# A short-convolution block on one core: two late operand forms split straight from PSUM, transposes of the second half spread between products, five late low parts spaced out

## The chip, the cores and the metric

The kernel runs on one core of a Trainium2 chip. The metric is the device time of one execution in microseconds. The median of three runs of the kernel before is 780.94 us (780.88 to 781.16).

## The reference, cut to what matters

The inputs are x of 1024 frames by 1024 channels, two norm weights, `w_in` (1024 x 8192), three taps for each of 2048 channels, and `w_out` (2048 x 1024), all float32. There is one layer, and its mixer is the short convolution:

```python
u = rms_norm(x, pre_norm)
z, bg, cg, v = jnp.split(u @ w_in, 4, axis=-1)      # 4 x 2048 columns
y = bg * causal_dwconv(cg * v, conv_w) * jax.nn.silu(z)
out = x + rms_norm(y @ w_out, post_norm)
```

## The kernel before, in words

**Precision.** Every float32 operand of a matmul is split into a high part (a rounded copy, made by ScalarE) and a low part (operand minus high part, made by VectorE or GpSimd). `pass3` (lines 122 to 125) multiplies low by high, high by low and high by high into one PSUM bank. So one product over one block of 128 input channels is three matmuls of 512 columns.

**The products.** The 64 column groups of `w_in` (16 channel blocks times four types: CG, V, Z, BG) are worked off in this way: the first four, called plain, by full products (`plain`, lines 511 to 521: 8 blocks of channels for each half of the frames, 24 matmuls for one group and half, accumulated in a bank `pp`). The other 60 are taken in 20 triples by a bilinear scheme: 20 products `product(t, i)` of six matmuls each replace the larger number of direct ones. The normalized and transposed x is held as eight blocks B[g, h] (g: four groups of 256 channels, h: two halves of 512 frames). Each of the 20 products has its own left operand, U[i]: seven products use a block B itself (lines 756 and 757; five blocks serve them), the other thirteen use "forms", sums and differences of blocks. A form is built once at the start, split into high and low, and used by all 20 triples.

**Where a form is built.** `form(i, ...)` (line 550) and `banks_of(i)` (line 718) build a form in two PSUM banks; `stage(i)` (line 538) is a place in SBUF for forms that are finished later. `high_u(i)` (line 555) allocates the operand tile u_i and makes the high part on ScalarE; `low_u(i)` (line 563) makes the low part on VectorE, or on GpSimd if told so. Each reads the form from its banks as long as it is listed in `FORM`, else from SBUF (line 569 instead of 567). `keep(i)` (line 578) copies a form from its banks to its staging place, so that the banks come free. Before the change forms 6 and 11 are kept in that way and split in the product loop; form 8 is one addition of two SBUF blocks (line 694).

**Order.** The order is written out by hand; each engine takes its instructions in that order. Lines 668 to 760 are the part that the change touches: while TensorE works on the plain products, x of the second half is transposed by TensorE in pairs of blocks (`turn2`, line 530, eight matmuls of 128 columns for a pair), read out with scale and split into B[g, 1] (`read_k`, line 473: line 479 on ScalarE, line 480 on VectorE), combined into staged forms (`turned`, line 585, issued at line 588), and written back as plain float32 (`rebuild_a`, line 488). `snap` (line 523) reads a finished plain bank with ScalarE.

The loop over triples (line 822) issues for each of 20 positions s: the six matmuls of one product, `read` of its bank (line 334: the first read of a group is a copy by ScalarE, lines 345 and 347, later ones an add or subtract by VectorE, lines 351 and 353), the outstanding low parts of weights (`run_lows`; lines 218 to 224 are the split of a unit of two weight operands, with the unit's name in the tile: wA to wJ), outstanding low parts of forms (`low_us`), and only in the first triple `first_chunk` and the late forms: at odd s one of `LATE` gets its high part, and its low part is issued one position later. The first triple's order of products is `ORDER_0` (line 820): 7, 9, 1, 8, 3, 5, 14, 18, 0, 13, 17, 6, 4, 11, 15, 16, 10, 2, 12, 19. Products of one chain (line 127: X, Y, V, Z, W) accumulate in one bank and are read in between, so a product waits for the reads of the chain's product before it.

**Space.** There are 8 PSUM banks (line 58), taken in turn as they come free, for transposes, plain sums, forms, weight splits and chains alike. The pool `up` has 18 slots (line 56). It holds the eight blocks B, the split plain weights wn0 to wn3 (`high_w`, line 503; each free after the plain products of its group on both halves), the operands u_i and four staging tiles s_0 to s_3, each with two forms (`PLACE`, line 536: 10 and 4, 0 and 16, 6 and 17, 11 and 2). In the end all 18 slots hold operands of products. The split weights' tiles and others of the product loop take the memory of the head's tiles xa and xb (line 741 closes that pool), so the first write to them waits for the last reader of xa, which is the building of form 2 at line 735.

## Time and profile before

| | |
|---|---|
| Median of three runs | 780.94 us (780.88 to 781.16) |
| The profiled execution's own time | 780.58 us |
| Its span, first to last instruction | 778.8 us |
| Mean granted TensorE clock over the span | 0.996 |
| Instructions | 10028 |

The span leaves 1.78 us of the profiled execution's time around it. The profile names engines PE (TensorE's matmuls), PEld (its weight loads), DVE (VectorE), ACT (ScalarE), POOL (GpSimd) and SP (SyncE). A row of the timeline has the start in us from the span's start, the duration, engine and line, output and inputs by the program's names, the number of merged instructions, and in brackets the idle time before them with what ended it. Matmul durations are of pipelined instructions, so two rows in turn overlap; their starts tell the pace.

### The profile page before, as it was taken

How to read it: one execution, taken by the hardware profiler on the slowest of the kernel's cores; microseconds unless marked ns; L12 is line 12 of the kernel's file. 1: busy time of each engine (PE TensorE's matmuls, PEld its weight loads, DVE VectorE, ACT ScalarE, POOL GpSimd, SP SyncE). 2: the span in 40 equal slices, each digit the busy share in tenths (PEclk: the TensorE clock that was granted, in tenths of full speed). 3: DMA queues.
4: the chain of work that ended last, by engine and by line, in shares of the span. 5: the costliest groups of instructions: out<-in, count | busy, mean ns of one | idle time of the engine just before them, and what ended most of it. 6: DMA issues, size and time to landing. Idle time of an engine off the chain costs nothing.

```text
span 778.8 us, 10028 instructions
## 1 busy us (share of the span) xinstructions
PE 763.1 (98%) x3394; PEld 629.3 (81%) x3394; DVE 490.6 (63%) x752; ACT 451.2 (58%) x879; POOL 460.0 (59%) x563
## 2 busy tenths in 40 slices
PE   8989899999999999999999999999999999999996
PEld 8877688888888888888888888888888888888885
DVE  6897865655566465656565665555664957544756
ACT  7749565666556566645665755565565636544531
POOL 0688487678669669676977986796884320000020
PEclk9999999999999999999999999999999999999999
DMA  9400325545535446356267366565544779754237
GB/s 331 131 0 28 108 68 163 121 125 138 144 96 162 135 109 187 82 156 151 79 138 195 76 177 128 147 159 113 129 104 133 233 241 375 282 189 176 99 118 260
DMA packets 103219, 116.55 MB, mean 150 GB/s; under 512 B 4680, under 2 KB 70272, under 8 KB 102144
## 3 DMA queue, kind: packets, MB, share of 16 engines
q1 hardware_dynamic: 93936, 99.13, 38.6%
q0 software_dynamic: 9216, 16.78, 13.8%
q8 instruction: 26, 0.43, 0.2%
q14 instruction: 25, 0.20, 0.1%
q10 hardware_dynamic: 16, 0.00, 0.0%
HBM read 97.02 MB, written 44.04 MB: 181 GB/s over the span
## 4 chain that ended last, share of the span: by engine, by line
PE 88%; ACT 6%; DVE 5%; issue 1%; DMA 0%; DVEq 0%; ACTq 0%
PE pX L123 8%; PE pX L125 8%; PE pX L124 8%; PE pY L123 7%; PE pY L124 7%; PE pY L125 7%; PE po_x L887 4%; PE po_x L886 4%; PE po_x L885 4%; PE pV L123 3%; PE pV L125 3%; PE pV L124 3%; PE pZ L123 2%; PE pZ L124 2%; PE pZ L125 2%; PE pW L123 2%
## 5 line engine op out<-in xcount | busy, mean ns | idle before, releaser
L925 POOL TENSOR_TENSOR res<-xr,res 128x512 f32<-128x512 f32 x4 | 6.9, 1720 | 105.4 <-DVE res L924 105.4
L329 POOL TENSOR_TENSOR g<-g,sn 128x512 f32<-128x512 f32 x29 | 40.1, 1390 | 46.0 <-ACT sn L327 35.4
L353 DVE TENSOR_TENSOR sn<-sn,pY 128x512 f32<-128x512 f32 x57 | 39.2, 688 | 35.9 <-PE pY L125 21.6
L353 DVE TENSOR_TENSOR sn<-sn,pX 128x512 f32<-128x512 f32 x57 | 39.2, 688 | 34.9 <-PE pX L125 34.9
L302 POOL TENSOR_TENSOR g<-sn,g 128x512 f32<-128x512 f32 x23 | 29.8, 1298 | 47.8 <-DVE sn L351 47.8
L327 ACT ACTIVATE sn<-sn 128x512 f32<-128x512 f32 x24 | 15.2, 632 | 64.1 <-DVE sn L353 40.1
L311 POOL TENSOR_TENSOR g<-g,sn 128x512 f32<-128x512 f32 x20 | 28.2, 1411 | 17.7 <-DVE sn L353 17.4
L345 ACT COPY sn<-pZ 128x512 f32<-128x512 f32 x19 | 11.2, 588 | 46.6 <-PE pZ L125 46.6
L347 ACT ACTIVATE sn<-pV 128x512 f32<-128x512 f32 x38 | 20.7, 599 | 28.6 <-PE pV L125 28.6
L169 POOL TENSOR_TENSOR raw<-raw 128x256 f32<-128x256 f32 x40 | 32.5, 929 | 0.0
L359 POOL DMA_DIRECT2D s_d<-s_d x24 | 19.8, 823 | 21.0 <-DMA s_d<-y_d 13.5
L174 POOL TENSOR_TENSOR raw<-e,raw 128x256 f32<-128x256 f32 x40 | 29.2, 751 | 1.6
L351 DVE TENSOR_TENSOR g<-pY,g 128x512 f32<-128x512 f32 x15 | 10.4, 692 | 30.7 <-PE pY L125 30.7
L123 PE MATMUL pp<-b,wn 128*128 128x512 f32 x64 | 25.9, 405 | 2.1 <-ACT b L479 1.8
L170 POOL TENSOR_TENSOR e<-raw,raw 128x512 f32<-128x512 f32 x20 | 25.8, 1292 | 1.6
L894 ACT ACTIVATE jk<-res 128x512 bf16<-128x512 f32 x12 | 7.6, 632 | 31.9 <-DVE res L952 13.0
L124 PE MATMUL pp<-b,wn 128*128 128x512 f32 x64 | 25.2, 394 | 0.6 <-DVE b L480 0.6
L125 PE MATMUL pp<-b,wn 128*128 128x512 f32 x64 | 25.0, 390 | 0.0
L292 DVE SCALAR_TENSOR_TENSOR g<-g,cw,cv 128x512 f32<-128x512 f32 x30 | 22.5, 749 | 1.7
L224 DVE TENSOR_TENSOR wD<-wD,wD 128x512 fp32r<-128x512 f32 x20 | 13.7, 685 | 14.8 <-ACT wD L223 14.8
L181 POOL TENSOR_TENSOR e<-e,raw 128x256 f32<-128x256 f32 x20 | 14.8, 740 | 13.9 <-ACT wB L219 13.9
L292 DVE SCALAR_TENSOR_TENSOR cv<-g,cw,cv 128x512 f32<-128x512 f32 x30 | 22.4, 748 | 0.0
(373 smaller groups left out, 2910.0 us busy)
## 6 DMA issues: line engine op xcount, KB each, us to landing
raw<-in_sc_w_in SPq DMA_DIRECT2D x64, 512.0 KB, 4.4
t_d<-in_sc_w_out SPq DMA_DIRECT2D x32, 256.0 KB, 4.3
s_d<-g SPq DMA_DIRECT2D x29, 256.0 KB, 2.1
s_d<-s_d POOLq DMA_DIRECT2D x24, 256.0 KB, 4.4
y_d<-g SPq DMA_DIRECT2D x23, 256.0 KB, 2.5
t_d<-in_sc_w_out POOLq DMA_DIRECT2D x16, 256.0 KB, 7.8
t_d<-t_d POOLq DMA_DIRECT2D x16, 256.0 KB, 4.3
xr<-in_x SPq DMA_DIRECT2D x8, 512.0 KB, 4.9
```

The lines of the kernel that those rows point to most:

```text
L123: nc.tensor.matmul(ps, lo, u[:, 0, kk], start=first, stop=False, skip_group_check=True)
L124: nc.tensor.matmul(ps, hi, u[:, 1, kk], start=False, stop=False, skip_group_check=True)
L125: nc.tensor.matmul(ps, hi, u[:, 0, kk], start=False, stop=last, skip_group_check=True)
L169: 0: lambda: (add(w2[:, 0], w2[:, 0], w2[:, 1]), add(w2[:, 2], w2[:, 1], w2[:, 2])),
L174: 5: lambda: (sub(w0[:, 2], e[:, 3], w0[:, 2]), sub(w0[:, 0], e[:, 3], w0[:, 0])),
L292: nc.vector.scalar_tensor_tensor(g if j == TAPS - 1 else ps, g, tap(c, j), ps, op0=ALU.mult, op1=ALU.add)
L302: nc.gpsimd.tensor_mul(g, src, g)
L329: when([(c, "cv", h), (c, "silu", h)], (c, "z", h), {"cv": 1, "silu": 1}, lambda: nc.gpsimd.tensor_mul(cv_of(c, h), cv_of(c, h), t))
L353: nc.vector.tensor_sub(a, a, ps)
L885: nc.tensor.matmul(ps, lo, u[:, 0, k % 2], start=first, stop=False, skip_group_check=True)
L886: nc.tensor.matmul(ps, hi, u[:, 1, k % 2], start=False, stop=False, skip_group_check=True)
L887: nc.tensor.matmul(ps, hi, u[:, 0, k % 2], start=False, stop=last, skip_group_check=True)
```

## The change

Form 8 gets its two banks earlier (`banks_of` moves up). ScalarE copies b20 (block of group 2, first half) into them, VectorE adds b00 in place, and high and low part follow at once, ahead of the transposes of the second half. The plain product of group 3 on the first half is no longer cut in two; it runs whole before the first pair of transposes. After each pair come products that need only blocks already read.

Forms 6 and 11 are no longer kept in SBUF: their high parts are made from the banks at once, the low part of 6 as soon as form 2 is staged, the low part of 11 behind the split of weight unit B. High and low part of form 0 move behind the first four weight units. The late list has five forms, 4, 16, 10, 2 and 19, at s = 4, 7, 10, 12 and 14, where there were seven at s = 1, 3, 5, 7, 9, 11 and 13.

```diff
@@ -578,6 +578,10 @@
+    def banks_of(i):
+        FORM[i] = [bank(f"f_{i}_{kk}") for kk in range(2)]
+        return in_bank(i)
@@ -673,17 +677,23 @@
     low_u(7)
     high_u(9)
     form(5, turned(4, gneg, b00, ALU.subtract), [pk[4, 1], pk[5, 1]])
+    f8 = banks_of(8)
+    for kk in range(2):
+        nc.scalar.copy(f8[kk], b20[:, kk])
     low_u(9)
     sn0[2] = snap(2, 0)
     high_u(5)
-    plain(3, 0, range(KH))
+    make(nc.vector, f8, "+", f8, b00)
+    low_u(5)
+    high_u(8)
+    low_u(8)
+    plain(3, 0, range(NK))
     turn2((0, 1))
     for k in (0, 1):
         read_k(k, 1)
     for kk in range(2):
         turned(0, gneg, b00, ALU.add)(stage(10)[:, kk], kk)
-    low_u(5)
-    plain(3, 0, range(KH, NK))
+    plain(0, 1, (4, 5))
     turn2((6, 7))
     for k in (0, 1):
         rebuild_a(k, 1)
@@ -691,20 +701,17 @@
         read_k(k, 1)
     for kk in range(2):
         turned(6, gcol, b30, ALU.subtract)(stage(4)[:, kk], kk)
-    form(8, lambda dst, kk: nc.vector.tensor_add(dst, b00[:, kk], b20[:, kk]))
+    plain(1, 1, (4, 5))
+    plain(0, 1, (0, 1))
+    turn2((2, 3))
     sn0[3] = snap(3, 0)
-    plain(0, 1, (4, 5, 0, 1))
-    turn2((2, 3))
-    high_u(8)
     for k in (6, 7):
         rebuild_a(k, 1)
-    low_u(8)
     for k in (2, 3):
         read_k(k, 1)
-    plain(0, 1, (6, 7))
-    plain(1, 1, (4, 5))
-    plain(0, 1, (2, 3))
-    plain(1, 1, (0, 1, 6, 7, 2, 3))
+    plain(1, 1, (0, 1))
+    plain(0, 1, (6, 7, 2, 3))
+    plain(1, 1, (6, 7, 2, 3))
     sums(0, range(12))
@@ -726,18 +729,18 @@
-    keep(6)
+    high_u(6)
     make(nc.vector, stage(17), "+", f6, b30)
     nc.vector.tensor_mul(cv_of(0, 1), plain_ps[1, 1], cv_of(0, 1))
     f11 = banks_of(11)
     make(nc.vector, f11, "-", f6, b00)
-    keep(11)
+    high_u(11)
     make(nc.vector, stage(2), "+", f11, b10)
-    FORM.clear()
+    FORM.pop(19)
+    FORM.pop("q")
+    low_u(6)
     nc.gpsimd.tensor_mul(inner(gts[0, 0]), inner(gts[0, 0]), sn0[1])
     pad(0)
-    high_u(0)
-    low_u(0, nc.gpsimd)
     head.close()
@@ -745,9 +748,12 @@
     for unit in "ABCD":
         split_w(0, unit)
         run_lows()
+        if unit == "B":
+            low_u(11)
     sums(0, range(12, 16))
-    high_u(17)
-    low_u(17, nc.gpsimd)
+    for i in (0, 17):
+        high_u(i)
+        low_u(i, nc.gpsimd)
     first_tap(0, 0)
@@ -755,7 +761,7 @@
-    LATE = [6, 4, 11, 16, 10, 2, 19]
+    LATE = [4, 16, 10, 2, 19]
@@ -829,7 +835,7 @@
             if t == 0:
                 first_chunk(s)
-                if s % 2 and LATE:
+                if s in (4, 7, 10, 12, 14):
                     n = LATE.pop(0)
                     high_u(n)
                     low_us.append(lambda n=n: low_u(n))
```

More of the change, by code (lines that the diff above doesn't have):

```diff
@@ L716 @@
         plain(n, 1, (4, 5, 0, 1, 6, 7, 2, 3))
-    def banks_of(i):
-        FORM[i] = [bank(f"f_{i}_{kk}") for kk in range(2)]
-        return in_bank(i)
     snap(0, 1, True)
```

## The prediction

> **What bounds the kernel now.** First the page, for shares and the chain that ended last.

> ```profile
> span 778.8 us, 10028 instructions
> PE 763.1 (98%) x3394; PEld 629.3 (81%) x3394; DVE 490.6 (63%) x752; ACT 451.2 (58%) x879; POOL 460.0 (59%) x563
> PE 88%; ACT 6%; DVE 5%; issue 1%; DMA 0%; DVEq 0%; ACTq 0%
> ```

> TensorE holds 88% of the chain; ScalarE and VectorE together hold 11%. The change removes no matmul, so only that 11% can shrink. Then the busy time by stretches, to find where it lies (columns: stretch, its length, busy time and instructions of PE, PEld, DVE, ACT and POOL, granted clock, DMA share, GB/s).

> ```profile
> 40.00:48.00 8.00, 7.72 (x41) 6.05 (x39) 7.80 (x12) 4.21 (x8) 7.84 (x9) 1.00 0.00 1
> 48.00:52.00 4.00, 2.05 (x9) 1.43 (x9) 2.95 (x5) 2.29 (x5) 4.00 (x4) 1.00 0.00 0
> 76.50:80.00 3.50, 1.34 (x6) 1.06 (x6) 3.50 (x5) 2.82 (x7) 3.38 (x6) 0.98 0.00 0
> 80.00:83.40 3.40, 3.40 (x10) 2.68 (x9) 3.40 (x5) 0.00 (x0) 3.40 (x4) 0.52 0.00 0
> 83.40:92.00 8.60, 7.21 (x30) 5.04 (x28) 7.55 (x12) 4.44 (x8) 3.78 (x4) 1.00 0.36 132
> 99.00:776.00 677.00, 672.66 (x2962) 555.32 (x2961) 411.48 (x617) 381.26 (x750) 402.63 (x498) 1.00 0.55 154
> ```

> From 99 us TensorE is full. Its holes lie at 48 to 52, at 76.5 to 80, in a half-clock stretch right behind, and up to 92 us: in the very part that the change touches. Then TensorE's own timeline.

> ```profile
> 33.69 0.39 PE L123 MATMUL pp<-b,wn 128*128 128x512 f32 x1
> 41.35 0.50 PE L123 MATMUL pp<-b,wn 128*128 128x512 f32 x1 [0.28 <-DVE u L567]
> 49.68 0.49 PE L123 MATMUL pp<-b,wn 128*128 128x512 f32 x1 [1.66 <-ACT b L479]
> 50.47 0.50 PE L124 MATMUL pp<-b,wn 128*128 128x512 f32 x1 [0.29 <-DVE b L480]
> 66.68 0.39 PE L123 MATMUL pV<-u,wA 128*128 128x512 f32 x1
> 72.12 0.39 PE L123 MATMUL pY<-b,wC 128*128 128x512 f32 x1
> 75.97 0.39 PE L125 MATMUL pV<-b,wD 128*128 128x512 f32 x1
> 78.66 0.50 PE L123 MATMUL pX<-b,wD 128*128 128x512 f32 x1 [2.30 <-DVE g L351]
> 85.37 0.50 PE L123 MATMUL pY<-u,wE 128*128 128x512 f32 x1 [0.71 <-ACT u L561]
> 89.06 0.50 PE L123 MATMUL pY<-u,wF 128*128 128x512 f32 x1 [0.67 <-DVE gc L353]
> 98.25 0.50 PE L123 MATMUL pX<-b,wJ 128*128 128x512 f32 x1
> ```

> Products begin at 66.68; 41 starts later it is 75.97, so a matmul costs 0.2266 us and a product of six 1.36. Product 18 waits until 78.66 for the read of product 5, product 17 until 85.37, and product 12, the last but one of the triple, starts at 98.25. Whatever the change gains is the amount by which that last start moves: nothing after it waits.

> VectorE's and ScalarE's rows say why.

> ```profile
> 33.37 1.28 DVE L567 TENSOR_TENSOR u<-f,u 128x512 fp32r<-128x512 f32 x2
> 44.68 2.58 DVE L694 TENSOR_TENSOR f<-xa 128x512 f32<-128x512 f32 x2
> 50.98 1.41 DVE L588 SCALAR_TENSOR_TENSOR f_q<-pk,gcol,xb 128x512 f32<-128x512 f32 x2
> 59.30 1.29 DVE L576 TENSOR_TENSOR s<-f,xa 128x512 f32<-128x512 f32 x2
> 72.35 5.06 DVE L569 TENSOR_TENSOR u<-s,u 128x512 fp32r<-128x512 f32 x4
> L569 DVE TENSOR_TENSOR u<-s,u x4: 1067/1218/1784, 72.3 to 76.2; 128x512 fp32r<-128x512 f32 x4
> 82.21 2.50 DVE L569 TENSOR_TENSOR u<-s,u 128x512 fp32r<-128x512 f32 x2
> 84.64 0.68 DVE L224 TENSOR_TENSOR wE<-wE,wE 128x512 fp32r<-128x512 f32 x1
> 90.66 1.28 DVE L569 TENSOR_TENSOR u<-s,u 128x512 fp32r<-128x512 f32 x2
> ...
> 32.44 2.04 ACT L559 CAST u<-f 128x512 fp32r<-128x512 f32 x4
> 34.50 1.28 ACT L527 ACT_TABLE_LOAD   x1
> 37.23 1.29 ACT L479 ACTIVATE b<-pk,gcol 128x512 fp32r<-128x512 f32 x2
> 41.32 1.26 ACT L479 ACTIVATE b<-pk,gcol 128x512 fp32r<-128x512 f32 x2
> 48.93 1.28 ACT L479 ACTIVATE b<-pk,gcol 128x512 fp32r<-128x512 f32 x2
> 61.55 0.59 ACT L223 CAST wA<-wA 128x512 fp32r<-128x512 f32 x1
> 68.24 1.09 ACT L347 ACTIVATE gc<-pV 128x512 f32<-128x512 f32 x2
> 84.75 1.14 ACT L561 CAST u<-s 128x512 fp32r<-128x512 f32 x2 [5.30 <-DVE u L569]
> ...
> 68.80 1.43 POOL L169 TENSOR_TENSOR raw<-raw 128x256 f32<-128x256 f32 x2
> 71.56 3.02 POOL L764 TENSOR_TENSOR sp<-sp,sp 128x512 f32<-128x512 f32 x2
> ```

> A subtraction from PSUM takes 1.28 for two halves (33.37). With both operands in SBUF it takes as little once GpSimd rests (90.66), but 2.50 (82.21) or 5.06 for four halves (72.35) while GpSimd works; so does the addition of form 8 (44.68, 2.58). [...]

> **The change part by part.** The walk uses the profiled execution's times. Pitches: 0.60 for VectorE in a pair (1.28 has one overlap), 0.66 with a scale (1.41), 0.51 for a copy by ScalarE (2.04 for four).

> *Form 8 early.* Gone are two additions of 2.58 together and ScalarE's wait for them. Added are two copies (2 x 0.51; SBUF to PSUM, between 0.49 and 0.62 each by the weight splits' like rows) and two additions into PSUM (2 x 0.60; up to 1.29 each if they too met GpSimd, which nothing that reads one PSUM operand does in the trace). ScalarE: high part of 9 done 34.48, copies 35.5, table load 36.8, snap 37.3, high of 5 38.35, high of 8 39.4. VectorE: form 5 done 35.9 (34.57 + 2 x 0.66), low of 9 37.1, additions 38.3, low of 5 39.5, low of 8 40.7. All this lies beside 24 plain matmuls (5.44 us); without that cover it would cost about 2 us.

> *A bank.* There are eight. Form 8 now takes the two that come free first: that of the transposed taps and the first of form 7. The plain sum of group 3 gets the second of form 7, free only when its low part ends, 33.37 + 1.28 = 34.65. TensorE would be there at 33.69 as now. **New wait: 1.0 us**; bounds 0 (another bank) and 3.8 (the bank of the sum before, read by snap until 37.5).

> *Transposes.* TensorE: 34.7 + 0.1 for the restart + 5.44 = 40.24 for the first pair, which ScalarE reads from 40.9. A pair costs the ping-pong of ScalarE and VectorE: read, low parts, staged form, write back, next read: 1.29 + 1.41 + 1.41 with their gaps, 4.09 from the read at 37.23 to the next pair's at 41.32. So the third pair is read at 40.9 + 2 x 4.09 = 49.1, against 48.93: nothing is won on that chain, as it starts later. But TensorE then has fewer matmuls left, for six of group 1 went ahead. Its second matmul on that pair comes 1.54 after the read (50.47 - 48.93), at 50.62, with 64 to follow before the products instead of 70: products can begin at 50.62 + 0.33 + 64 x 0.2266 = **65.46, a gain of 1.2**. On the other side of the pair, VectorE's chain of forms starts at 51.13, 0.15 late.

> *Forms 6 and 11.* The copies that kept them become high parts of the same length. VectorE's low parts, 2 x 1.2 us, fall where it idles now, between 60.6 and 66.3. But u_6 and u_11 now take two of the 18 slots before the staging tiles of 17 and 2. Free by then: B[2,0], wn0, wn1, wn2 in that order. Form 2 gets the fourth, wn2, free when the plain sum of group 2 ends on the second half: 24 matmuls before the products, 65.46 - 5.44 + 0.2 = 60.25. VectorE would have come at 59.45 (59.30 + 0.15). So form 2 ends at 61.55, and the third copy of unit A on ScalarE, which writes where form 2's operand lies, waits for it until 61.6, against 60.7 that it could (form 0's high part, 1.04, no longer stands ahead). ScalarE then runs without a pause: A, B, C, D, high of 0 and 17, the taps. Its two copies of product 7's bank come at 69.35 instead of 68.24. **Product 8 waits for them until 70.45, and product 3 starts at 72.0 against 72.12 now: the 1.2 is spent, 0.1 is left.** Bounds: no wait for a slot, 0.95 more gain; another slot, below.

> GpSimd makes the low part of 0 after the four sums that follow unit B, 66.3 to 68.85; product 0 needs it at 80. All of these issue no DMA; SP's later loads of weights come when raw slots free, no later than now.

> *Five late ones.* Ahead of the read of product 5 stands one low part (form 4) instead of two. ScalarE: unit F 71.75, copy 72.25, high of 4 73.3, unit G 74.35. VectorE: low of G 75.05, then low of 4. GpSimd's two long multiplications (L764), ready after the taps, sit at 74.2 to 77.2: the two halves meet them and cost 1.07 + 1.78, the least and most of the first four. End 77.9, read 78.5: **product 18 at 78.55, against 78.66.** Its wait is as long as now, so the half clock follows again: matmul starts 0.43 apart. Then: 18 ends 80.0, read 80.75, low of H 81.35, low of 16 83.85 (2.50), low of E 84.45, product 17 at **84.5 against 85.37**. The half clock on products 0 and 13 is hidden in that. From there the backlog is shorter by two low parts: read of 17 at 86.75 (needed 87.2), of 4 at 89.7 (needed 90.0), of 10 at 95.2 (needed 95.45). No wait is left: eight products from 84.5 + 0.1 give 95.45 for product 12, against 98.25.

> **Sum: 2.8 us**, 0.87 of it at product 17 and 1.9 from the waits behind it. The profiled execution's 780.58 becomes 777.8; it stands 0.36 under the median 780.94, so the forecast is **778.1**.

> [...] The trace saw the fall behind 2.30 us; the half clock lasted from 80.0 to 83.4.

> **The rivals.**

> 1. *The new waits don't come* (other bank, other slot): product 17 is 0.95 to 1.9 earlier: 777.1 down to 776.2. For it: the bank and slot order is read from code and from one wait (41.35, which names the low part that freed a bank), not seen. Chance 0.13.

> 2. *VectorE's queue stays the bound.* If the half clock begins 1.4 us sooner it falls on product 18, whose read is waited for: six matmuls at 0.43 cost 1.2. [...] If every low part in SBUF up to unit E takes 1.78 a half, it is 4 x 1.78 - 2.85 - 2.50 = 1.8. So 779.3 to 781.1. For it: product 18 keeps its wait. Against: 1.78 is the largest seen. This is also the case in which the change misses its own aim. Chance 0.22.

> 3. *Slower: form 2's staging waits for a slot that only group 3's second half frees*, if one slot fewer is free than I count. Then it starts at 65.7, not 60.25; VectorE and ScalarE stand behind it, product 7 waits, everything later shifts by 5.45: 783.5. It decides from a start later than 63.1 (60.25 + 2.8). For it: 18 slots all in use at that moment. Against: the count above leaves wn2. Chance 0.10.

> **How the numbers follow.** The forecast has 0.55, with its own range 777.2 to 779.3 (0.9 and 1.2 either way, the size of one wait). Under 0.2% (1.56 us), a measurement can't tell from no change, so faster means under 779.4: the forecast, rival 1 and 0.05 of rival 2: 0.73. Same: the rest of rival 2, 0.17. Slower: rival 3, 0.10. The range 776.4 to 780.8 leaves out rival 3, and a little of 1 and 2.

> **What would show it.** TensorE waits about 1 us near 33.7 for a low part (L567); its wait near 50 is under 0.9; VectorE waits before form 2 (the second `make` on s) for a plain matmul; product 8 waits for ScalarE's copies; product 18 waits 2 us or more; product 12 starts near 95.5; PSUM low parts take 0.64 a half. I am wrong if product 18 doesn't wait (more gain), or if the wait before form 2 reaches past 63.

## The result

The changed kernel takes 777.9 us (median of 12 runs, 776.99 to 779.28) against 780.92 us for the kernel before, run beside it. The ratio is 0.9965, with a 95% interval of 0.9955 to 0.9974: 0.35% faster. The forecast was 778.1, the range 776.4 to 780.8. (One of twelve executions of the kernel before took 1565.1 us and is in no comparison.)

The profiled execution of the changed kernel took 776.99 us, the shortest of its twelve. Its page, in the same three lines as before:

```profile
span 775.2 us, 10034 instructions
PE 761.8 (98%) x3394; PEld 628.3 (81%) x3394; DVE 486.2 (63%) x752; ACT 451.1 (58%) x877; POOL 458.4 (59%) x563
PE 91%; ACT 5%; DVE 3%; issue 1%; DMA 0%; DVEq 0%; ACTq 0%
```

TensorE's share of the chain grew by 3 points, which ScalarE and VectorE lost. The stretches in which the kernel before had its holes (columns as before: stretch, length, busy time and instructions of PE, PEld, DVE, ACT and POOL, clock, DMA, GB/s):

```profile
48.00:52.00 4.00, 3.71 (x16) 2.63 (x15) 2.66 (x5) 2.26 (x5) 4.00 (x4) 1.00 0.00 0
76.00:79.50 3.50, 1.54 (x7) 1.10 (x7) 2.82 (x3) 2.19 (x5) 3.46 (x5) 1.00 0.00 0
79.50:83.00 3.50, 3.35 (x14) 2.13 (x12) 3.12 (x5) 0.00 (x0) 3.42 (x5) 1.00 0.00 0
83.00:91.60 8.60, 8.03 (x35) 6.50 (x36) 8.05 (x13) 6.85 (x14) 5.37 (x6) 1.00 0.65 202
```

The hole near 50 us is nearly shut (3.71 of 4.00 busy, 2.05 before), the one near 77 is still open, the stretch behind it has the full clock (0.52 before), and the last one is fuller. TensorE's timeline:

```profile
34.48 0.47 PE L123 MATMUL pp<-b,wn 128*128 128x512 f32 x1 [0.95 <-DVE u L567]
50.32 0.50 PE L124 MATMUL pp<-b,wn 128*128 128x512 f32 x1 [0.29 <-DVE b L480]
65.23 0.39 PE L123 MATMUL pV<-u,wA 128*128 128x512 f32 x1
70.28 0.50 PE L123 MATMUL pV<-u,wC 128*128 128x512 f32 x1 [0.80 <-ACT gc L347]
78.18 0.50 PE L123 MATMUL pX<-b,wD 128*128 128x512 f32 x1 [1.96 <-DVE g L351]
83.57 0.50 PE L123 MATMUL pY<-u,wE 128*128 128x512 f32 x1 [0.69 <-DVE wE L224]
94.69 0.39 PE L123 MATMUL pX<-b,wJ 128*128 128x512 f32 x1
```

Here are both new waits, for a bank (34.48) and for ScalarE's copies (70.28), the old wait of product 18, a shorter one of product 17, and product 12 at 94.69 instead of 98.25. VectorE's rows, then two of ScalarE's and one of GpSimd's:

```profile
33.06 1.28 DVE L567 TENSOR_TENSOR u<-f,u 128x512 fp32r<-128x512 f32 x2
60.09 1.29 DVE L576 TENSOR_TENSOR s<-f,xa 128x512 f32<-128x512 f32 x2 [1.11 <-PE pp L125]
61.30 1.28 DVE L567 TENSOR_TENSOR u<-f,u 128x512 fp32r<-128x512 f32 x2
63.74 1.28 DVE L567 TENSOR_TENSOR u<-f,u 128x512 fp32r<-128x512 f32 x2
74.80 2.73 DVE L569 TENSOR_TENSOR u<-s,u 128x512 fp32r<-128x512 f32 x2
81.08 1.83 DVE L569 TENSOR_TENSOR u<-s,u 128x512 fp32r<-128x512 f32 x2
88.97 1.28 DVE L569 TENSOR_TENSOR u<-s,u 128x512 fp32r<-128x512 f32 x2
...
48.80 1.26 ACT L479 ACTIVATE b<-pk,gcol 128x512 fp32r<-128x512 f32 x2
61.47 0.59 ACT L223 CAST wA<-wA 128x512 fp32r<-128x512 f32 x1 [1.14 <-DVE s L576]
...
73.99 2.99 POOL L770 TENSOR_TENSOR sp<-sp,sp 128x512 f32<-128x512 f32 x2
```

The low parts of forms 6 and 11 take 1.28 from their banks (61.30 and 63.74). Form 2 waits 1.11 for a plain matmul (60.09), and unit A's third copy 1.14 for form 2 (61.47). The low part of form 4 still meets GpSimd's long multiplications (74.80: 2.73, against 1.28 for two halves at 88.97, with GpSimd at rest).

### The profile page after: what moved, and what is told of

Its sections match the earlier page's. It is cut to its first block, busy times and chain, and to the rows that moved or that the text cites. A ratio compares the mean times of both kernels' runs of the same rounds, so it can differ in the third digit from the quotient of the medians.

```text
span 775.2 us, 10034 instructions
## 1 busy us (share of the span) xinstructions
PE 761.8 (98%) x3394; PEld 628.3 (81%) x3394; DVE 486.2 (63%) x752; ACT 451.1 (58%) x877; POOL 458.4 (59%) x563
## 4 chain that ended last, share of the span: by engine, by line
PE 91%; ACT 5%; DVE 3%; issue 1%; DMA 0%; DVEq 0%; ACTq 0%
PE pX L123 8%; PE pX L125 8%; PE pX L124 8%; PE pY L123 7%; PE pY L125 7%; PE pY L124 7%; PE po_x L892 4%; PE po_x L893 4%; PE po_x L891 4%; PE pV L123 3%; PE pV L125 3%; PE pV L124 3%; PE pZ L125 2%; PE pZ L123 2%; PE pZ L124 2%; PE pW L125 2%
## 5 line engine op out<-in xcount | busy, mean ns | idle before, releaser
L353 DVE TENSOR_TENSOR sn<-sn,pY 128x512 f32<-128x512 f32 x57 | 39.2, 688 | 36.2 <-PE pY L125 20.7
L353 DVE TENSOR_TENSOR sn<-sn,pX 128x512 f32<-128x512 f32 x57 | 39.2, 689 | 34.5 <-PE pX L125 34.5
L347 ACT ACTIVATE sn<-pV 128x512 f32<-128x512 f32 x38 | 20.7, 600 | 28.5 <-PE pV L125 28.5
L169 POOL TENSOR_TENSOR raw<-raw 128x256 f32<-128x256 f32 x40 | 32.6, 933 | 0.0
L351 DVE TENSOR_TENSOR g<-pY,g 128x512 f32<-128x512 f32 x15 | 10.4, 692 | 30.7 <-PE pY L125 30.7
L123 PE MATMUL pp<-b,wn 128*128 128x512 f32 x64 | 26.0, 406 | 1.1 <-DVE u L567 1.0
L124 PE MATMUL pp<-b,wn 128*128 128x512 f32 x64 | 25.2, 394 | 0.6 <-DVE b L480 0.6
L125 PE MATMUL pp<-b,wn 128*128 128x512 f32 x64 | 25.0, 390 | 0.0
L224 DVE TENSOR_TENSOR wD<-wD,wD 128x512 fp32r<-128x512 f32 x20 | 13.7, 684 | 14.3 <-ACT wD L223 14.3
```

What stands on the lines that cost most here:

```text
L123: nc.tensor.matmul(ps, lo, u[:, 0, kk], start=first, stop=False, skip_group_check=True)
L124: nc.tensor.matmul(ps, hi, u[:, 1, kk], start=False, stop=False, skip_group_check=True)
L125: nc.tensor.matmul(ps, hi, u[:, 0, kk], start=False, stop=last, skip_group_check=True)
L169: 0: lambda: (add(w2[:, 0], w2[:, 0], w2[:, 1]), add(w2[:, 2], w2[:, 1], w2[:, 2])),
L353: nc.vector.tensor_sub(a, a, ps)
```

## The experiments

Starts can be compared across runs from the first transposes of the second half on, since the head differs by up to 0.6 us from execution to execution. This table has, from each trace, that first start, and how long after it products 7, 18, 17 and 12 start; product 12's is what decides. A half clock is a stretch in which the granted clock reads 0.5 (0.52 or 0.53 as the mean of a stretch of 3.41 us); the last column leaves out the end of the kernel, past 770 us, where the traces of before (from 776.14) and of after (from 773.66) both have one.

The ratio of each run is to the kernel before, run beside it. That kernel's median lay between 780.36 and 780.92 in the different groups of runs, so two medians out of different groups tell nothing below some 0.6 us. early_only, late_only, one_stage and bank_first are one group; fill_wait, low4_later, bank_used_first and all_three the second; the last three rows of the table the third.

| run | first transposes | 7 | 18 | 17 | 12 | half clock in this trace |
|---|---|---|---|---|---|---|
| before | 26.95 | 39.73 | 51.71 | 58.42 | 71.30 | yes, hidden |
| after | 26.62 | 38.61 | 51.56 | 56.95 | 68.07 | no |
| early_only | 26.89 | 38.58 | 51.81 | 58.53 | 71.41 | yes, hidden |
| late_only | 27.23 | 41.24 | 54.17 | 60.16 | 71.42 | yes, on plain products |
| one_stage | 26.93 | 38.58 | 50.63 | 57.85 | 68.90 | yes, on product 18 |
| bank_first | 26.68 | 38.57 | 51.50 | 57.47 | 68.71 | yes, behind 18 |
| fill_wait | 27.02 | 38.53 | 51.48 | 56.87 | 67.97 | no |
| low4_later | 27.02 | 38.56 | 49.39 | 56.11 | 67.23 | no |
| bank_used_first | 26.98 | 37.55 | 50.47 | 56.46 | 67.69 | no |
| all_three | 27.06 | 37.49 | 47.45 | 54.17 | 65.28 | no |
| late_only_filled | 26.89 | 39.94 | 52.92 | 58.30 | 69.43 | no |
| before_filled | 26.91 | 39.88 | 51.89 | 58.62 | 71.50 | no |
| all_three_low4_last | 26.99 | 37.49 | 47.45 | 51.85 | 68.43 | yes, on product 12 |

The theory under test is the prediction's: the in-order work of ScalarE and VectorE sets the end, TensorE's early start is spent in new waits, and the gain lies in the last third of the first triple. The rival: the gain is that of matmuls started earlier and low parts taken out of GpSimd's way, and the new waits are slack.

**The early part alone.** The kernel before, with these edits and the changed order of plain products and transposes:

```diff
+    f8 = banks_of(8)
+    for kk in range(2):
+        nc.scalar.copy(f8[kk], b20[:, kk])
...
+    make(nc.vector, f8, "+", f8, b00)
+    low_u(5)
+    high_u(8)
+    low_u(8)
+    plain(3, 0, range(NK))
...
-    form(8, lambda dst, kk: nc.vector.tensor_add(dst, b00[:, kk], b20[:, kk]))
```

> Only the early part of the change: form 8 split before the transposes, transposes spread; forms 6 and 11 kept in SBUF and the seven late forms as before. Theory (the chain of ScalarE and VectorE sets the end, TensorE's earlier start is lost again): products begin some 1.2 us earlier than before, but the chain of forms starts no earlier (within 0.2), so product 18 and product 12 start where they did, within 0.3 us: 780.4 to 781.3. Rival (TensorE's progress counts as such, the parts add up): 1.2 us less than before, 779.7.

Measured: 780.64 us, ratio 1.0005 (0.9996 to 1.0014). TensorE's and VectorE's rows of that run:

```profile
78.70 0.50 PE L123 MATMUL pX<-b,wD 128*128 128x512 f32 x1 [3.32 <-DVE g L351]
98.30 0.50 PE L123 MATMUL pX<-b,wJ 128*128 128x512 f32 x1
...
72.37 5.08 DVE L569 TENSOR_TENSOR u<-s,u 128x512 fp32r<-128x512 f32 x4
```

Products begin 1.15 us earlier (38.58 against 39.73 in the table), and product 18 simply waits 3.32 instead of 2.30: four halves of low parts stand ahead of the read that it needs (72.37, 5.08). The rival's 779.7 is out. Alone, 1.15 us of earlier matmuls are worth nothing.

**The late part alone.** The other edits:

```diff
-    keep(6)
+    high_u(6)
...
-    keep(11)
+    high_u(11)
...
+    low_u(6)
...
+        if unit == "B":
+            low_u(11)
...
-    LATE = [6, 4, 11, 16, 10, 2, 19]
+    LATE = [4, 16, 10, 2, 19]
```

> Only the late part: forms 6 and 11 split from their banks, five late forms; form 8, plain products and transposes in the order of before. Theory: the wait for the slot of the split weights of group 2 lasts longer than in the whole change, since TensorE frees it 1.2 us later: form 2 starts at about 61.4 in the trace instead of 60.1, and everything behind it is 1.2 us later than with the whole change, so the gain is 1.6 to 2.0 instead of 2.8 to 3.2: about 779.1. Rival (the parts are independent): all of the gain but 1.2, the same number, but form 2 starts without a wait at 59.3 and the loss is in TensorE's late start of the products (66.7).

Measured: 780.88 us, ratio 0.9999 (0.9990 to 1.0009), with single runs from 778.27 to 781.56. That is a miss of both numbers. Its trace, TensorE's rows and VectorE's form 2 first, then two stretches of 3.41 us:

```profile
49.93 0.50 PE L123 MATMUL pp<-b,wn 128*128 128x512 f32 x1 [1.62 <-ACT b L479]
51.73 0.63 PE L123 MATMUL pp<-b,wn 128*128 128x512 f32 x1
63.33 1.29 DVE L576 TENSOR_TENSOR s<-f,xa 128x512 f32<-128x512 f32 x2 [3.64 <-PE pp L125]
...
47.28:50.69 3.41, 1.53 (x6) 0.71 (x4) 2.30 (x5) 2.91 (x5) 3.41 (x3) 0.98 0.00 0
50.69:54.10 3.41, 3.38 (x8) 2.71 (x9) 3.41 (x6) 0.85 (x2) 3.41 (x4) 0.52 0.00 0
```

Behind TensorE's wait near 50 comes a half-clock stretch on plain products, where nothing hides it. It delays the plain sum that frees form 2's slot, so form 2 starts at 63.33 and not 61.4. The kernel before has the same wait near 50 (1.66 us, 1.62 here); in its trace the clock stayed full there (1.00 from 48 to 52). To try this cause, late_only_filled puts matmuls into the two waits (one VectorE instruction, early on, makes the zero operand):

```diff
+    for _ in range(7):
+        nc.tensor.matmul(plain_ps[1, 1], zero, B[2, 1][:, 0, 0], start=False, stop=False, skip_group_check=True)
     plain(0, 1, (2, 3))
...
-        if first:
+        if first and (t, ch) not in banks:
...
+        if (t, i) == (0, 18):
+            banks[0, "W"] = bank("pW_0")
+            for _ in range(8):
+                nc.tensor.matmul(banks[0, "W"], x[:, 0, :P], U[14][:, 0, 0], start=True, stop=True, skip_group_check=True)
```

> The late part alone, plus extra matmuls in TensorE's two long waits: seven ahead of the plain products on the last pair of blocks (with a zero operand, added to an open sum) and eight ahead of product 18 (results not used). Theory (late_only's missing gain went into half-clock stretches that follow those waits): no half clock, 778.2 to 779.3, spread under 0.7. Rival (the late part alone gives nothing without the early one): 780.5 to 781.

Measured: 778.49 us (778.31 to 779.31), ratio 0.9973 (0.9962 to 0.9985).

```profile
66.83 0.39 PE L123 MATMUL pV<-u,wA 128*128 128x512 f32 x1
96.32 0.40 PE L123 MATMUL pX<-b,wJ 128*128 128x512 f32 x1
```

With 15 matmuls more, the late part is 2.4 us faster than without them: the half clock had eaten its gain. Product 12 stands 1.36 later than with the whole change (69.43 against 68.07), close to the 1.2 that theory gave for the missing early part.

**The kernel before, with the same filling.** The same edit on the kernel before.

> The kernel before, with the same extra matmuls in the same two waits. Theory: the half-clock stretch goes here too, but it was hidden behind the wait of product 17 for VectorE, so the time stays within 0.3 of the kernel before. Rival (the half clock costs its 1.7 us wherever it falls): 778.9.

Measured: 780.82 us, ratio 1.0003 (0.9994 to 1.0012).

```profile
85.53 0.50 PE L123 MATMUL pY<-u,wE 128*128 128x512 f32 x1 [1.38 <-ACT u L565]
98.41 0.50 PE L123 MATMUL pX<-b,wJ 128*128 128x512 f32 x1
```

The half clock is gone, and product 17 waits longer instead (1.38; 0.71 before) and starts where it did. In the kernel before the half clock cost nothing. Its other runs say the same. A mean granted clock of 0.999 leaves no room for a half clock of 3.41 us ahead of the end, which alone takes 0.002 off the mean (half of 3.41 us in a span of 778.8). Beside the first two groups of experiments 31 runs of the kernel before are on record (the 17 of the third group have none at 0.999): the eight at 0.999 took 780.22 to 781.12 us, the 23 at 0.995 or 0.996 took 780.01 to 780.81.

**Filling the wait of product 18 in the changed kernel.** The second half of that edit, on the changed kernel.

> The whole change, plus eight extra matmuls ahead of product 18 in the wait that it has there, into the bank that product 0 clears afterwards; their results are not used. Nothing on another engine changes. Theory (a half-clock stretch follows when TensorE idles for about half of one 3.41 us clock window, and it is what spreads the runs with the change from 777.0 to 779.3): TensorE no longer idles over 1 us in any window, no half clock falls ahead of the last matmul, all runs between 776.9 and 777.7. Rival (the spread has another source, or the extra matmuls only lengthen the way): runs up to 779.3 remain, or the median grows.

Measured: 777.26 us, all runs between 777.01 and 777.49, ratio 0.9956 (0.9943 to 0.9968).

```profile
78.50 0.50 PE L123 MATMUL pX<-b,wD 128*128 128x512 f32 x1
94.99 0.39 PE L123 MATMUL pX<-b,wJ 128*128 128x512 f32 x1
```

Product 18 starts without an idle time and no earlier; the runs' spread of 2.29 us shrinks to 0.48. All five runs lie under 777.5, where five of twelve did without the filling. The median is 0.6 us lower, but it is of another group and the two intervals overlap, so a gain in the median is not shown. That the spread comes from a half clock behind product 18's wait fits this, and it fits the twelve runs of the change: the five with a mean clock of 0.999 took 776.99 to 777.48 us, the seven at 0.995 to 0.997 took 777.67 to 779.28. It isn't all: in bank_first, further on, which is a repeat of the change, two runs at 0.999 took 777.96 and 777.99, and four at 0.995 or 0.996 took 777.59 to 778.97.

**One staging tile fewer.** Forms 17 and 2 share a tile, so a slot is free for form 2.

```diff
-    PLACE = {10: (0, 0), 4: (0, 1), 0: (1, 0), 16: (1, 1), 6: (2, 0), 17: (2, 1), 11: (3, 0), 2: (3, 1)}
+    PLACE = {10: (0, 0), 4: (0, 1), 0: (1, 0), 16: (1, 1), 17: (2, 0), 2: (2, 1)}
```

> The whole change, and forms 17 and 2 share one staging tile, so that a slot is free and form 2 need not wait for the plain sum of group 2. Theory: the wait of 1.1 us before form 2 goes, ScalarE's chain is 1.1 earlier, product 8 doesn't wait, products 18, 17 and 12 start 0.9 to 1.1 us earlier: 1.0 us less than with the change. Rival (that wait was slack, the gain came from low parts out of PSUM alone): no difference, within 0.3.

Measured: 777.16 us (776.22 to 778.05), ratio 0.9960 (0.9947 to 0.9972): by time alone not apart from the change. The trace decides:

```profile
59.46 1.29 DVE L576 TENSOR_TENSOR s<-f,xa 128x512 f32<-128x512 f32 x2 [0.18 <-ACT u L559]
77.56 0.76 PE L123 MATMUL pX<-b,wD 128*128 128x512 f32 x1 [1.98 <-DVE g L351]
...
74.36:77.77 3.41, 1.43 (x7) 0.89 (x6) 3.31 (x4) 3.14 (x8) 3.41 (x4) 0.98 0.00 0
77.77:81.18 3.41, 3.41 (x9) 2.67 (x10) 1.22 (x3) 0.00 (x0) 3.29 (x7) 0.52 0.00 0
```

Form 2 no longer waits for TensorE (59.46), product 8 neither, and product 18 starts 0.93 earlier (50.63 against 51.56 in the table), as theory said. Then the half clock falls on product 18 itself, and product 17 is 0.90 later than with the change. Of the 1.0 expected, 0.8 shows against bank_first, the repeat of the change in the same group (777.98), and the two ranges of times overlap.

**The bank, twice.** First the plain sum's bank was asked for ahead of form 8's.

```diff
-            first = (n, h) not in plain_ps
-            if first:
+            first = plain_k.get((n, h), 0) == 0
+            if (n, h) not in plain_ps:
...
+    plain_ps[3, 0], plain_k[3, 0] = bank("pp_3_0"), 0
     f8 = banks_of(8)
```

> The whole change, but the plain sum of group 3 takes its bank before form 8 does. Theory: TensorE's wait of 0.95 near 34 goes; transposes, the chain of forms and the end of the plain sum that frees form 2's slot all come 0.6 to 1.0 earlier, and so does product 12: 0.6 to 1.0 us less than with the change. Rival (TensorE's early wait is made up behind, because the pairs of transposes are bound by ScalarE and VectorE): no difference, within 0.3.

Measured: 777.98 us (777.59 to 778.97), ratio 0.9972 (0.9960 to 0.9983). The list of waits still holds the one that should have gone:

```profile
PE pp L123 <- DVE u L567: 0.9, 1, 0.9
```

So the edit didn't do what it was for. As this run and the next show it, what counts is where a bank is first used, not where it is asked for. The run is a repeat of the change, with the half clock in its trace and product 12 0.64 later than in the trace of the change. The second try writes the first three matmuls of that sum ahead of form 8's copies:

```diff
+    plain(3, 0, range(1))
     f8 = banks_of(8)
...
-    plain(3, 0, range(NK))
+    plain(3, 0, range(1, NK))
```

> The whole change, with the first three matmuls of the plain sum of group 3 written ahead of form 8's copies, so that this sum takes the free bank and form 8 waits for the two of form 7. The order on each engine stays. Theory: TensorE's wait of 0.95 near 34 goes, and product 12 comes 0.6 to 1.0 earlier: 0.6 to 1.0 less than with the change. Rival (made up behind): no difference within 0.3.

Measured: 776.90 us (776.03 to 776.99), ratio 0.9950 (0.9937 to 0.9962), 1.0 less than the change's median, but in another group and with overlapping intervals; it is 0.36 less than fill_wait beside it.

```profile
77.45 0.50 PE L123 MATMUL pX<-b,wD 128*128 128x512 f32 x1 [1.94 <-DVE g L351]
94.67 0.39 PE L123 MATMUL pX<-b,wJ 128*128 128x512 f32 x1
```

The wait near 34 is gone, and products 7 and 18 start 1.06 and 1.09 earlier; of that 0.38 is left at product 12. The rival of no difference is out for the start of 18, and nearer the truth for the end.

**Form 4's low part behind the read.** One number:

```diff
-                if s in (4, 7, 10, 12, 14):
+                if s in (5, 7, 10, 12, 14):
```

> The whole change, but the high part of form 4 at s = 5 instead of 4, so that its low part stands behind the read of product 5 and not ahead of it. Theory: product 18 doesn't wait, starts near 75.9 instead of 78.2, product 17 near 82.0 instead of 83.6, product 12 1.3 to 1.8 us earlier; no half clock: 775.3 to 776.2 with little spread. Rival (the low part costs the same wherever it stands, as VectorE is full up to unit E): product 17 starts where it did, only the half clock goes: 777.2.

Measured: 776.62 us (776.54 to 776.65), ratio 0.9948 (0.9935 to 0.9960). No half clock, almost no spread, but less gain than expected: product 18 starts 2.17 earlier and product 12 only 0.84. TensorE's waits and VectorE's row say why:

```profile
PE pW L123 <- DVE wH L224: 1.1, 1, 1.1
PE pY L123 <- DVE wE L224: 1.1, 1, 1.1
...
75.93 2.64 DVE L569 TENSOR_TENSOR u<-s,u 128x512 fp32r<-128x512 f32 x2
```

The low part (2.64) now stands ahead of unit H's, for which product 13 waits, and then product 17 for unit E's. VectorE's queue is the bound there; the order moves the wait.

**All three together.** The shared tile, the bank by first use, and form 4's low part later.

> The bank used first, forms 17 and 2 in one staging tile, and form 4's low part behind the read of product 5, together. Theory: 0.8 + 1.0 + 1.5 us off the change's 777.2 of its runs without half clock: 774.0 to 775.2, little spread. Rival (they shorten the same chain once): 775.5 to 776.2, the best of the three alone.

Measured: 774.60 us (774.44 to 774.77), ratio 0.9922 (0.9909 to 0.9936): faster than both kernels, 0.8% under the one before.

```profile
PE 92%; DVE 3%; ACT 3%; issue 1%; DVEq 0%; ACTq 0%
...
81.23 0.50 PE L123 MATMUL pY<-u,wE 128*128 128x512 f32 x1 [1.06 <-DVE wE L224]
92.34 0.39 PE L123 MATMUL pX<-b,wJ 128*128 128x512 f32 x1
```

Product 12 starts 2.79 earlier than with the change (65.28 against 68.07). The three waits lay one behind the other on one chain, so their removals add: product 18 starts 4.11 earlier, and 0.93, 1.09 and 2.17 for the three alone make 4.19. At product 12 the sum can't be made from the single runs, as one of them had a half clock there.

**The low parts of units H and E ahead of form 4's.** The same, with the late forms at other places:

```diff
-                if s in (5, 7, 10, 12, 14):
+                if s in (8, 9, 11, 13, 14):
```

> All three edits of the run all_three, with the late forms at s = 8, 9, 11, 13 and 14, so that the low parts of weight units H and E stand ahead of form 4's. Theory (VectorE is full from product 5's read to the end of the triple; only what waits changes): products 13 and 17 don't wait, product 4 or 15 waits instead, product 12 starts 0 to 0.8 earlier than in all_three: 773.8 to 774.6. Rival (each wait removed counts): 2.1 less, 772.5.

Measured: 778.59 us (777.65 to 779.52), ratio 0.9973 (0.9961 to 0.9984): 4 us slower than all_three, a miss of theory and rival. TensorE's row and two of ScalarE's:

```profile
95.42 0.50 PE L123 MATMUL pX<-b,wJ 128*128 128x512 f32 x1 [2.01 <-DVE gc L353]
...
87.11 1.14 ACT L561 CAST u<-s 128x512 fp32r<-128x512 f32 x2 [2.37 <-DVE u L569]
91.56 1.14 ACT L561 CAST u<-s 128x512 fp32r<-128x512 f32 x2 [2.01 <-DVE u L569]
```

Products 13 and 17 don't wait any more (17 starts at 51.85 in the table, 54.17 in all_three). But two late high parts need the slots that the low parts before them free: ScalarE stands 2.37 and 2.01 for that, with weight unit J and then units of the next triple queued behind. VectorE, which was counted as full, stands still for 1.36 (before unit J's low part) and 0.74 (before the low part made from the row at 91.56). That low part is ahead of the read for which product 12 waits 2.01, with a half clock on its heels. The runs separate the two costs: the three with a mean clock of 0.998 or 0.999 took 777.65 to 777.78, the three at 0.996 or 0.997 took 779.41 to 779.52. So some 3 us against all_three are the chain of slots, which the sum left out, and another 1.8, in half of the runs, the half clock; the median lies between the two.

## Why the prediction was right, and where it was not

The median is 0.2 us under the forecast, but two errors of size cancel in that. Times of the change are given 0.33 later here, to stand on the clock of the trace of before (26.95 - 26.62).

- *The bank:* 1.0 foretold, 0.95 found, for the low part named. Right, and bank_used_first shows that it is worth 1.06 at product 7.
- *The transposes:* third pair read at 49.13 (49.1 foretold), its second matmul at 50.65 (50.62), products from 65.56 (65.46). Right.
- *Forms 6 and 11:* low parts 1.28 each pair in VectorE's idle time, form 2 at 60.42 after a wait for the plain sum (60.25), product 8 at 70.61 (70.45), product 3 at 72.19 (72.0). Right; one_stage shows that the slot is the cause.
- *Five late ones:* product 18 at 78.51 (78.55). Right. **Mis-sized:** the low part of 16 was put at 2.50 and took 1.83. GpSimd had two sums of 256 columns beside it (from 81.11 and 82.33 in its trace), where before it had one of 512 and two of 256; that this is the cause was not tried. Product 17 came at 83.90 instead of 84.5 and product 12 at 95.02 instead of 95.45. The gain of the walk is 3.23, not 2.8.
- *The half clock:* **this step failed.** The prediction let it follow the wait of 18 again and hid it behind the wait of 17. It doesn't follow in every execution: this profile has none, one_stage and bank_first have it. Where it comes it isn't wholly hidden: 17's own wait shrank to 0.69, and in bank_first product 17 came 0.52 and product 12 0.64 later than in the trace of the change. Times: 777.26 with the wait filled, up to 779.28 without. The slowest runs of the change lie 1.8 above those at a clock of 0.999, more than these 0.64; they have no trace, so where their half clock fell is open. Rival 2 had a half clock on product 18 itself; that it could begin 1.4 us sooner was the author's assumption, and one_stage's trace shows one from 77.77, with product 18 at 77.56. That the median came out 0.2 from the forecast is luck: the walk's gain was 0.43 too small, and the half clock, taken as free, was not.
- *The rivals:* the new waits did come, so rival 1 is out. Rival 3 is out: wn2's slot was free at 60. In late_only, which had the same wait with TensorE later, form 2 started at 63.33 (63.05 on the clock of before), and the gain was gone as rival 3's turning point (63.1) has it.
- *PSUM or SBUF as the source:* two halves with the form in PSUM took 1.28 (61.30 and 63.74), the 0.64 a half foretold; two with both operands in SBUF and GpSimd at rest took 1.28 as well (88.97). These rows show no cost of the PSUM source.

Not tried: a kernel in which the low parts of 6 and 11 read from SBUF at their new places, which would weigh the PSUM source against the place. The trace speaks for the place in one of the two: GpSimd did nothing from 53.7 to 63.18, so the low part of 6 (61.30 to 62.58) had nobody to get out of the way of. early_only and late_only_filled tell what the early and the late half of the change are worth, not this.

## What to carry to other kernels

Follow each engine's queue and each pool's slots through the edited stretch before adding up: here the four new waits (TensorE for a bank, VectorE for a slot, ScalarE for form 2, product 8 for the copies) ended within 0.2 us of where a sum from rows of the old trace had them, and a gain of 1.15 us in matmuls started earlier was worth nothing (early_only, ratio 1.0005) until the queue behind it was shorter. When a wait's cover shrinks, ask what else it was covering: the kernel before hid a half-clock stretch for nothing (before_filled, which has none, has a ratio of 1.0003), the changed one pays for it in some executions (product 12 came 0.64 later in bank_first). Where a short TensorE wait can't be removed, matmuls whose result nobody reads can be worth their place, as in the late part alone (780.88 without them, 778.49 with).

## What the runs showed of the hardware

The half clock lasted 3.41 us each time (in early_only this is read from eight matmul starts 0.43 us apart, 79.55 to 82.53, as in before from 80.00 to 82.99), and came after a stretch of 3.41 us in which TensorE was busy for 0.82 (early_only), 1.26 (before), 1.40 (all_three_low4_last), 1.43 (one_stage), 1.45 (bank_first) and 1.53 us (late_only). Below are a row of all_three_low4_last, two of late_only, nine stretches of 3.41 us behind its row at 47.28, and two of the change, cut where its own half clock at the end puts the grid:

```profile
92.65:96.06 3.41, 1.40 (x6) 0.80 (x5) 3.41 (x7) 3.30 (x8) 0.82 (x2) 0.97 0.28 81
...
77.98:81.39 3.41, 1.46 (x7) 0.88 (x5) 3.37 (x4) 3.28 (x8) 3.41 (x4) 1.00 0.00 0
81.39:84.81 3.42, 3.41 (x14) 2.49 (x15) 2.39 (x4) 0.10 (x1) 3.30 (x6) 1.00 0.00 0
...
74.03:77.44 3.41, 2.19 (x10) 1.49 (x8) 3.25 (x3) 3.32 (x9) 3.41 (x4) 1.00 0.07 19
77.44:80.85 3.41, 2.67 (x12) 2.18 (x12) 2.35 (x5) 0.82 (x2) 3.29 (x6) 1.00 0.00 0
```
